# Griffin-style block on one core: another home for one weight load, and the scheduler's order for the block products on TensorE

## The chip, the cores and the metric

The kernel runs on one core of one Trainium2 chip. The metric is the device time of one execution in microseconds (us), lower is better; a run's figure is that of the core, and several runs are given as a median with their lowest and highest. The engines are TensorE (PE: matmuls; PEld is its weight load), VectorE (DVE), ScalarE (ACT), GpSimd (POOL) and SyncE (SP, which here issues the weight loads). Each has its own instruction stream and takes it in order; the streams wait for each other through semaphores.

## The reference

One layer of a streaming encoder, batch 1, 512 frames, width 1024, everything in float32:

```python
xn = rmsnorm(h, norm_mix_g[l])
u = jnp.einsum('bsd,de->bse', xn, w_in[l])
q, k, v, xr, gr, ga, gb = jnp.split(u, splits, axis=-1)
ya = chunked_band_attention(q, k, v, rel_table[l]) @ w_attn_out[l]
xc = causal_depthwise_conv(xr, conv_w[l], conv_b[l])
hr = rg_lru(xc, w_rg_r[l], b_rg_r[l], w_rg_i[l], b_rg_i[l], rg_lambda[l])
yb = (hr * jax.nn.gelu(gr)) @ w_rnn_out[l]
gates = jax.nn.sigmoid(jnp.concatenate([ga, gb], axis=-1) + b_merge[l])
g_a, g_b = jnp.split(gates, 2, axis=-1)
h = h + (g_a * ya + g_b * yb) @ w_o[l]
hn = rmsnorm(h, norm_ffn_g[l])
gu = hn @ w_ffn_in[l]
g, up = jnp.split(gu, 2, axis=-1)
h = h + (jax.nn.silu(g) * up) @ w_ffn_out[l]
return rmsnorm(h, final_norm_g)
```

The change lies in `gu = hn @ w_ffn_in`: 512 x 1024 times 1024 x 5632, that is 22 column tiles of 128 for the gate half (g) and 22 for the up half (u).

## The kernel before, in words

**Products.** Every float32 operand is split into a high part (an ACT copy to a rounded type, L80) and a low part (source minus high part on DVE, L81), in the function `split`. A product is then three matmuls per 128 rows of the contraction: high x high, high x low, low x high (`mm3`, L74 to L76).

**Stages in the order of time.** Norm and input projection, recurrence, attention, the merge into `mT`, the product with `w_o` (po_h), the second norm (`norm_half`), the first FFN column pair fg0 and fu0 done plainly (po_f), then the block products fg2, fu2, fg4, fu4 ... fg20, fu20, and the output product (po_out) with the final norm.

**Block products.** From the second pair of column tiles on, a 1024 x 256 piece of weights is cut into 2 x 2 blocks (a11, a21, a12, a22), and hn into b11, b12, b21, b22. Sums of weight blocks (s1 to s4, `weight_sums`, L175 to L181) and of hn blocks (t1 to t4, L971) let seven block products do the work of eight. Each is 4 x 3 = 12 matmuls of 128x256 (`product`). `block_product` issues the seven in this order, with two PSUM banks:

- p takes a11 x b11, and later, added onto it, s2 x t2, s3 x t3 and a22 x t4. Between them ACT copies the bank's running value out (`keep`, L274): twice into `keepa`, once into `keepb`, and at the end into c[:, 2].
- q holds two halves: a12 x b21 in the first; s1 x t1 and, on top of it, s4 x b22 in the second. After s1 ACT keeps the second half in `keepb`.
- DVE adds keeps and q into the result c (L286, L287). `keepa` and `keepb` are the two buffers of the tag `tg`, so the next block's keeps wait for these additions.

The order is p a11, q a12, p s2, q s1, p s3, q s4, p a22. A running value must be copied before the next product may write the bank. p has four buffers (tag mm, shared with po_f), q two for g and two for u.

After the g block, ACT applies silu to c (L1020); after the u block, DVE multiplies (L1022). Before the last pair (j = 20), `split_act(0)` starts splitting the finished activations for po_out (L1008 on ACT, L1009 on POOL).

**Weights.** `prefetch` and `weights` build a block's weights one block ahead in the program text. `load` (L137 to L152) brings a raw block of 512 KB by a DMA on SP, two per piece: `raw_fg_0` holds a11 and a21, `raw_fg_4` holds a12 and a22. Raw blocks live in the pool `wp`, tag raw, three buffers; every fourth load of the block products (L145) goes to the pool `sc` instead (`room[0]`), which has one buffer for it. The split blocks live in four buffers of `wp` plus one in `sums`, a22 in two of `sc`. For fg2 the sums are made early: `weight_sums("fg2", True)` loads both blocks once for the sums (loads 1 and 2), and later, after `sc` is opened, both blocks are loaded again for a11, a12 and a22 (loads 3 and 4); these three go to buffers of the pool `act`. Load 4, fg2's second raw block, therefore lies in `sc`. `sc` is opened after `x32` is closed and takes over its place, where a half of hn lies that po_f reads.

**Order.** A scheduler orders each engine's instructions when the program is built. Where the text stands in `tc.manual_schedule(engines={PE})`, TensorE keeps the order of the text; the loop over the block products (L1013 to L1022) stands in such a block. ACT, DVE and SP are ordered by the scheduler there too. Pools decide who waits: a tile waits until its buffer's last user is done.

Of the kernel before, what the change touches and what calls it, by code (L numbers as in the profile page):

```python
# [8 lines left out]
F32 = mybir.dt.float32  # L9
F32R = mybir.dt.float32r  # L10
AF = mybir.ActivationFunctionType
# [3 lines left out]
P = 128  # L15
# [7 lines left out]
FT = DFF // P  # L23
# [13 lines left out]
def block_kernel(ctx: ExitStack, tc: tile.TileContext, x, norm_mix_g, w_in, b_merge, rel_table,  # L37
# [3 lines left out]
    pe, dve, act, pool, sp = nc.tensor, nc.vector, nc.scalar, nc.gpsimd, nc.sync  # L41

    def pool_of(name, bufs=1, side="left"):
        return tc.tile_pool(name=name, bufs=bufs, side=side, reuse_waits="tile")

    def opened(name, bufs=1, side="left"):
        st = ExitStack()
        return st, st.enter_context(pool_of(name, bufs, side))
# [6 lines left out]
    wp = ctx.enter_context(pool_of("wp", 2))  # L55
# [10 lines left out]
    def f(ap):  # L66
        return ap.bitcast(F32)
# [69 lines left out]
    def load(name, k):  # L137
        _, parts, rows, kts = chunks[index[name]]
        wide = sum(width for *_, width in parts)
        n = min(4 * CW // wide, kts - k)  # L140
        at = rows + k * P
        pl, bufs = wp, 3
        if name in strassen and name[0] == "f":
            loads[0] += 1
            pl, bufs = (room[0], 1) if loads[0] % 4 == 0 else (wp, 3)  # L145
        raw = pl.tile([P, n, wide], F32, tag="raw", bufs=bufs, name=f"raw_{name}_{k}")
        to = 0
        for src, col, width in parts:
            sp.dma_start(out=raw[:, :, to:to + width],
                         in_=src[at:at + n * P, col:col + width].rearrange("(k p) e -> p k e", p=P))  # L150
            to += width
        raws[name, k] = raw  # L152

    slots, loads = [0], [0]
    barrier = ["wo1"]
    room = [None]
# [4 lines left out]
    def weight_sums(name, ahead=False):  # L161

        def blocks_of():
            for k in (0, 4):
                if (name, k) not in raws:
                    load(name, k)
            r0, r1 = raws.pop((name, 0)), raws.pop((name, 4))
            return r0[:, :, 0:P], r0[:, :, P:CW], r1[:, :, 0:P], r1[:, :, P:CW]
# [51 lines left out]
    def prefetch(n):  # L220
        while len(made) < min(n, len(chunks), index.get(barrier[0], len(chunks))):
            name, parts, rows, kts = chunks[len(made)]
            if name in strassen:
                made.append(weight_sums(name))
                continue
            tiles = []
            wide = sum(width for *_, width in parts)
            step = 4 * CW // wide
            for k in range(0, kts, step):
                n_ = min(step, kts - k)  # L230
                if name in extra:
                    hl = extra[name].tile([P, 2, n_, wide], F32R, tag="whl", bufs=4, name=f"whl_{name}_{k}")
                else:
                    hl = wp.tile([P, 2, n_, wide], F32R, tag="whl", bufs=4, name=f"whl_{name}_{k}")
                if (name, k) not in raws:
                    load(name, k)
                raw = raws.pop((name, k))
                split(hl[:, 0], hl[:, 1], raw[:])
                tiles.append(hl)
            made.append(lambda part, k, at, tiles=tiles, step=step: tiles[k // step][:, part, k % step, at])  # L240

    def weights(name, ahead=1):
        prefetch(index[name] + 1 + ahead)
        return made[index[name]]
# [10 lines left out]
    def right_side(blk_at, sums):  # L255
        out = {f"b{kh + 1}{half + 1}": lambda part, k, kh=kh, half=half: blk_at(kh, half, part, k)
               for kh in range(2) for half in range(2)}
        out.update({f"t{i + 1}": lambda part, k, i=i: sums[i][:, part, k] for i in range(4)})
        return out

    def product(o, w, b, start):

        for k in range(4):
            mm3(o, w[:, 0, k], w[:, 1, k], b(0, k), b(1, k), start and k == 0, k == 3, parts=True)

    def block_product(name, i, right, c):

        w = weights(name)
        p = ps.tile([P, 256], F32, tag="mm", bufs=4, name=f"p_{name}")
        q = ps.tile([P, 2, 256], F32, tag="st"[i % 2], bufs=2, name=f"q_{name}")  # L270
        a, b = (tg_.tile([P, 2, 256], F32, tag="tg", name=f"keep{n}_{name}") for n in "ab")

        def keep(o, src):
            act.activation(o, src, AF.Copy)  # L274

        product(p[:], w["a11"], right["b11"], True)
        keep(a[:, 0], p[:])
        product(q[:, 0], w["a12"], right["b21"], True)
        product(p[:], w["s2"], right["t2"], False)
        keep(a[:, 1], p[:])  # L280
        product(q[:, 1], w["s1"], right["t1"], True)
        keep(b[:, 0], q[:, 1])
        product(p[:], w["s3"], right["t3"], False)
        keep(b[:, 1], p[:])
        product(q[:, 1], w["s4"], right["b22"], False)
        dve.tensor_add(c[:, 3], b[:, 0], b[:, 1])  # L286
        dve.tensor_add(c[:, 0:2], q[:], a[:])  # L287
        product(p[:], w["a22"], right["t4"], False)
        keep(c[:, 2], p[:])
# [17 lines left out]
    warm = cp.tile([P, 1], F32, name="warm")  # L307
    act.activation(warm[:], eps_t[:], AF.Sqrt)
    load("xr0", 0)
    load("xr0", 4)  # L310
    for t in range(2, NT):
# [280 lines left out]
    def gelu_in(j, po_gr):  # L592

        g = rw.tile([P, S], F32, tag="g", name=f"g{j}")
        act.activation(g[:], po_gr[:], AF.Square, scale=(GELU_C * GELU_A) ** 0.5)
        dve.scalar_tensor_tensor(g[:], g[:], GELU_C, po_gr[:], ALU.add, ALU.mult)
        return g
# [77 lines left out]
    with tc.manual_schedule(engines={mybir.EngineType.Activation, mybir.EngineType.DVE}):  # L675
# [8 lines left out]
        g = [gelu_in(0, po[0])]  # L684
# [253 lines left out]
    def act_tile(j):  # L938
        o = acp.tile([P, 2, S], F32, tag="act", name=f"act{j}")
        act2.append(o)  # L940
        return o
# [40 lines left out]
    for i, t in enumerate((t1, t2, t3, t4)):  # L982
        o = btp.tile([P, 2, 4, 256], F32R, name=f"bt{i}")
# [3 lines left out]
    hn_right = right_side(lambda kh, half, part, k: bl[kh, half][:, part, k], bt)  # L987
    x32_stack.close()
    sc_stack, sc = opened("sc", 2)
# [13 lines left out]
    def split_act(i):  # L1003
        o = act2[i]
        pl, bufs = (acp, 13) if i == 0 else (ohp, 6) if i < 7 else (op, 4)
        hi = pl.tile([P, 2, S], F32R, tag="act", bufs=bufs, name=f"act_hi{i}")
        lo = acp.tile([P, 2, S], F32R, tag="act", bufs=13, name=f"act_lo{i}")
        act.activation(hi[:], o[:], AF.Copy)  # L1008
        (pool if i in (0, 1, 2, 4) else dve).tensor_sub(lo[:], o[:], f(hi[:]))  # L1009
        for c in range(2):  # L1010
            actT[2 * i + c] = (hi[:, c], lo[:, c])

    with tc.manual_schedule(engines={mybir.EngineType.PE}):  # L1013
        for j in range(2, FT, 2):
            if j == FT - 2:
                split_act(0)
            g, u = (sc.tile([P, 4, 256], F32, tag=f"c{w}", name=f"c_{w}{j}") for w in "gu")
            block_product(f"fg{j}", 0, hn_right, g)
            o = act_tile(j)[:].rearrange("p a b -> p (a b)")
            act.activation(o, g[:].rearrange("p a b -> p (a b)"), AF.Silu)  # L1020
            block_product(f"fu{j}", 1, hn_right, u)
            dve.tensor_mul(o, o, u[:].rearrange("p a b -> p (a b)"))  # L1022
    sc_stack.close()
    bt_stack.close()
    sums_stack.close()
# [100 lines left out]
```

## Time and profile before

| | us |
|---|---|
| median of 3 runs | 883.68 |
| lowest, highest | 883.22, 884.0 |
| the profiled execution's own time | 883.01 |
| its span, from the first to the last instruction | 881.2 |
| TensorE busy | 869.5 |
| VectorE busy | 552.1 |
| ScalarE busy | 475.4 |
| GpSimd busy | 113.6 |

The profile is that of one execution. Times within it count from the span's start. A row of a timeline gives start, duration, engine, line, operation, out<-in, shapes, and in brackets how long the engine stood idle before it and what ended that. Matmuls are pipelined: one that lasts 0.28 us is followed by the next after 0.12 us, so a gap shows in the distance between two starts. In a row by stretches there follow, after the stretch's length, busy time and number of instructions of PE, PEld, DVE, ACT and POOL, then the granted TensorE clock, the DMA share and GB/s. A row of groups gives count, busy time and mean ns, then the engine's idle time before these instructions and what ended it. The mean granted TensorE clock of the execution is 0.998.

### The profile page before, as it was taken

The numbers are of one execution on the slowest core, as the hardware profiler recorded it, in microseconds if no ns is written. First come the engines' busy times: TensorE is split into PE (matmuls) and PEld (weight loads), VectorE is DVE, ScalarE is ACT, GpSimd is POOL, SyncE is SP. The second block draws the span as 40 slices with busy tenths as digits, with TensorE's granted clock in tenths as the row PEclk, the third lists the DMA queues.
The fourth block names the chain that finished last, engine by engine and source line by source line (L and its number), as shares of the span: only waits on it lengthen the run. The fifth ranks groups of instructions, "written<-read, shape, count | busy, mean of one in ns | idle before, by whom it ended". The sixth has DMA issues, their size and how long they took to land.

```text
span 881.2 us, 13339 instructions
## 1 busy us (share of the span) xinstructions
PE 869.5 (99%) x5220; PEld 775.8 (88%) x5220; DVE 552.1 (63%) x843; ACT 475.4 (54%) x827; POOL 113.6 (13%) x172
## 2 busy tenths in 40 slices
PE   9999999999999999999999999999999999999997
PEld 7988888888889888898888889899999999888886
DVE  5676556663456675766556458888888885564203
ACT  7586556642257675766534366655565665723103
POOL 3512112120112131312000000000000000401100
PEclk9999999999999999999999999999999999999999
DMA  8133222433332332322224531433333332363002
GB/s 287 54 120 100 91 91 79 119 96 96 107 108 73 86 94 73 107 87 61 96 90 151 190 96 46 146 97 98 119 96 108 109 96 73 96 212 121 26 1 96
DMA packets 86143, 90.10 MB, mean 102 GB/s; under 512 B 5456, under 2 KB 74672, under 8 KB 86080
## 3 DMA queue, kind: packets, MB, share of 16 engines
q1 hardware_dynamic: 84480, 85.73, 31.5%
q10 hardware_dynamic: 1376, 3.47, 1.0%
q8 instruction: 41, 0.67, 0.3%
q14 instruction: 22, 0.18, 0.1%
q0 software_dynamic: 224, 0.05, 0.0%
HBM read 87.10 MB, written 2.14 MB: 101 GB/s over the span
## 4 chain that ended last, share of the span: by engine, by line
PE 94%; DVE 2%; DMA 1%; ACT 1%; POOL 1%; issue 1%; DVEq 0%; POOLq 0%; ACTq 0%
PE po_out L75 5%; PE po_out L76 5%; PE po_out L74 5%; PE p_fu L74 2%; PE p_fu L76 2%; PE p_fu L75 2%; PE p_fg L74 2%; PE p_fg L76 2%; PE p_fg L75 2%; PE pT L806 2%; PE o L826 2%; PE po_v L74 2%; PE po_v L76 2%; PE po_v L75 2%; PE po_xr L75 2%; PE po_xr L74 2%
## 5 line engine op out<-in xcount | busy, mean ns | idle before, releaser
L75 PE MATMUL po_out<-whl_fo,act_hi 128*128 128x512 f32 (+1 forms) x198 | 72.4, 366 | 0.0
L74 PE MATMUL po_out<-whl_fo,act_hi 128*128 128x512 f32 (+1 forms) x198 | 72.4, 366 | 0.0
L76 PE MATMUL po_out<-whl_fo,act_lo 128*128 128x512 f32 (+1 forms) x198 | 71.7, 366 | 0.0
L81 DVE TENSOR_TENSOR whl_fo<-raw_fo,whl_fo 128x1024 fp32r<-128x1024 f32 x22 | 28.8, 1317 | 49.1 <-ACT whl_fo L80 48.6
L795 POOL TENSOR_SCALAR p<-p,rl 128x128 f32<-128x128 f32 (+1 forms) x64 | 36.7, 592 | 134.6 <-DVE rl L793 134.3
L1009 POOL TENSOR_TENSOR act_lo<-act,act_hi 128x1024 fp32r<-128x1024 f32 x4 | 11.3, 2836 | 328.4 <-PE q_fu L76 298.8
L80 ACT ACTIVATE whl_fo<-raw_fo 128x1024 fp32r<-128x1024 f32 x22 | 23.1, 1058 | 47.2 <-PE po_out L76 31.1
L74 PEld LDWEIGHTS po_out<-whl_fo,act_hi 128*128 128x128 f32 x198 | 37.4, 189 | 6.0
L76 PEld LDWEIGHTS po_out<-whl_fo,act_lo 128*128 128x128 f32 x198 | 37.3, 189 | 6.0
L75 PEld LDWEIGHTS po_out<-whl_fo,act_hi 128*128 128x128 f32 x198 | 37.4, 189 | 6.0
L792 ACT ACTIVATE p<-p,m 128x128 f32<-128x128 f32 (+1 forms) x64 | 35.7, 560 | 12.1 <-DVE m L791 11.8
L74 PE MATMUL po_v<-whl_v,xnT 128*128 128x256 f32 x128 | 36.5, 285 | 0.0
L76 PE MATMUL po_v<-whl_v,xnT 128*128 128x256 f32 x128 | 36.2, 283 | 0.0
L75 PE MATMUL po_v<-whl_v,xnT 128*128 128x256 f32 x128 | 36.2, 283 | 0.0
L81 DVE TENSOR_TENSOR whl_fg_s<-s_fg,whl_fg_s 128x1024 fp32r<-128x1024 f32 x20 | 25.6, 1281 | 11.8 <-ACT whl_fg_s L80 11.8
L80 ACT ACTIVATE whl_fu_s<-s_fu 128x1024 fp32r<-128x1024 f32 x20 | 21.1, 1059 | 20.9 <-PE q_fg L76 9.5
L80 ACT ACTIVATE whl_fg_s<-s_fg 128x1024 fp32r<-128x1024 f32 x20 | 21.2, 1058 | 18.6 <-PE q_fg L76 9.5
L791 DVE CUSTOM_DVE_ANT_0 p<-s,bias 128x128 f32<-128x128 f32 (+1 forms) x64 | 29.1, 483 | 1.0 <-PE s L783 1.0
L81 DVE TENSOR_TENSOR whl_qk<-raw_qk,whl_qk 128x1024 fp32r<-128x1024 f32 x16 | 20.9, 1305 | 13.4 <-ACT whl_qk L80 13.4
L81 DVE TENSOR_TENSOR whl_fu_s<-s_fu,whl_fu_s 128x1024 fp32r<-128x1024 f32 x20 | 24.4, 1225 | 5.6 <-ACT whl_fu_s L80 5.3
L81 DVE TENSOR_TENSOR pp<-pT,pp 128x384 fp32r<-128x384 f32 (+1 forms) x48 | 27.5, 596 | 0.5 <-ACT pp L80 0.4
L75 PE MATMUL po_xr<-xnT,whl_xr 128*128 128x512 f32 (+1 forms) x80 | 27.7, 353 | 0.0
(428 smaller groups left out, 3070.2 us busy)
## 6 DMA issues: line engine op xcount, KB each, us to landing
raw_fg<-in_w_ffn_in_dram SPq DMA_DIRECT2D x24, 512.0 KB, 3.5
raw_fu<-in_w_ffn_in_dram SPq DMA_DIRECT2D x22, 512.0 KB, 3.5
raw_fo<-in_w_ffn_out_dram SPq DMA_DIRECT2D x22, 512.0 KB, 3.5
raw_qk<-in_w_in_dram SPq DMA_DIRECT2D x32, 256.0 KB, 3.2
raw_xr<-in_w_in_dram SPq DMA_DIRECT2D x8, 512.0 KB, 3.5
raw_gr<-in_w_in_dram SPq DMA_DIRECT2D x8, 512.0 KB, 3.5
raw_ga<-in_w_in_dram SPq DMA_DIRECT2D x8, 512.0 KB, 3.5
raw_gb<-in_w_in_dram SPq DMA_DIRECT2D x8, 512.0 KB, 3.5
```

The lines of the kernel that those rows point to most:

```text
L74: pe.matmul(o, sh, mh, start=start, stop=False, skip_group_check=parts)
L75: pe.matmul(o, sh, ml, start=False, stop=False, skip_group_check=parts)
L76: pe.matmul(o, sl, mh, start=False, stop=stop, skip_group_check=parts)
L80: act.activation(hi, src, AF.Copy)
L81: dve.tensor_sub(lo, src, f(hi))
L791: dve.tensor_tensor_reduce(prob[qb][:], scs[qb][:, 0:w], bias[:, S - w:S], -1.0, 3e38, ALU.add, ALU.min, nmax[:, qb:qb + 1])
L792: act.activation(prob[qb][:], prob[qb][:], AF.Exp, bias=nmax[:, qb:qb + 1], scale=-1.0, accum_out=lsum[:, qb:qb + 1])
L795: pool.tensor_scalar(prob[qb][:], prob[qb][:], rl[:, qb:qb + 1], 1.0, ALU.mult, ALU.mult)
L806: pe.transpose(pt[:, at * P:(at + 1) * P], prob[qb][:, kb * P:(kb + 1) * P], ident[:])
L826: pe.matmul(po[:, S - n:S], st, pp[i][:, part, lo:lo + n], start=kb == 0 and part == 0, stop=kb == NT - 1 and part == 1)
L1009: (pool if i in (0, 1, 2, 4) else dve).tensor_sub(lo[:], o[:], f(hi[:]))
```

## The change

Two edits. In `load`, the fourth load of the block products no longer goes to `sc`; it takes a buffer of `wp` like its neighbours. Loads 8, 12, 16 and so on go to `sc` as before. In the loop over the block products, `manual_schedule` goes, so that the scheduler orders TensorE there too; the body of the loop is the same.

```diff
@@ -142,7 +142,7 @@
         pl, bufs = wp, 3
         if name in strassen and name[0] == "f":
             loads[0] += 1
-            pl, bufs = (room[0], 1) if loads[0] % 4 == 0 else (wp, 3)
+            pl, bufs = (room[0], 1) if loads[0] % 4 == 0 and loads[0] > 4 else (wp, 3)
         raw = pl.tile([P, n, wide], F32, tag="raw", bufs=bufs, name=f"raw_{name}_{k}")
@@ -1010,16 +1010,15 @@
-    with tc.manual_schedule(engines={mybir.EngineType.PE}):
-        for j in range(2, FT, 2):
-            if j == FT - 2:
-                split_act(0)
-            g, u = (sc.tile([P, 4, 256], F32, tag=f"c{w}", name=f"c_{w}{j}") for w in "gu")
-            block_product(f"fg{j}", 0, hn_right, g)
...
+    for j in range(2, FT, 2):
+        if j == FT - 2:
+            split_act(0)
+        g, u = (sc.tile([P, 4, 256], F32, tag=f"c{w}", name=f"c_{w}{j}") for w in "gu")
+        block_product(f"fg{j}", 0, hn_right, g)
...
```

In the built program the number of instructions on each engine is the same. TensorE's order is the same up to the first block product and again from the end of the last one. In between, the products of two or three blocks are woven into each other, for instance at the start: fg2 p a11 (12 matmuls), fg2 q a12 (12), fg2 q s1 (12), fu2 p a11 (4), fg2 p s2 (12), fu2 p a11 (8), fu2 q a12 (9), fg2 q s4 (12). SP's loads at this place stood in the order fg2 first, fu2 first, fu2 second, fg4 first, fg2 second, fg4 second; now fg2 first, fg2 second, fu2 first, fu2 second, fg4 first, fg4 second. The orders of ACT and DVE change in the same stretch.

More of the change, by code (lines that the diff above doesn't have):

```diff
@@ L1011, in split_act @@
             actT[2 * i + c] = (hi[:, c], lo[:, c])
-    with tc.manual_schedule(engines={mybir.EngineType.PE}):
-        for j in range(2, FT, 2):
-            if j == FT - 2:
-                split_act(0)
-            g, u = (sc.tile([P, 4, 256], F32, tag=f"c{w}", name=f"c_{w}{j}") for w in "gu")
-            block_product(f"fg{j}", 0, hn_right, g)
[L1019 to L1022, printed above, removed]
+    for j in range(2, FT, 2):
[3 more added lines that the diff above has]
+        block_product(f"fg{j}", 0, hn_right, g)
+        o = act_tile(j)[:].rearrange("p a b -> p (a b)")
+        act.activation(o, g[:].rearrange("p a b -> p (a b)"), AF.Silu)
+        block_product(f"fu{j}", 1, hn_right, u)
+        dve.tensor_mul(o, o, u[:].rearrange("p a b -> p (a b)"))
     sc_stack.close()
```

## The prediction

> **What bounds the kernel now.** I read the page's shares first, then the chain that ended last, then TensorE's waits, then the block-product stage (549 to 753 us) in stretches, and at last the matmuls around each gap.
>
> ```profile
> span 881.2 us, 13339 instructions
> ...
> PE 869.5 (99%) x5220; PEld 775.8 (88%) x5220; DVE 552.1 (63%) x843; ACT 475.4 (54%) x827; POOL 113.6 (13%) x172
> ...
> PE 94%; DVE 2%; DMA 1%; ACT 1%; POOL 1%; issue 1%; DVEq 0%; POOLq 0%; ACTq 0%
> ```
>
> TensorE is busy 99% of the span and carries 94% of the chain. The edit removes no matmul, so it can only win where TensorE stands still. What it waited for (total, times, longest, in us), for the rows in this stage:
>
> ```profile
> PE q_fg L74 <- ACT whl_fg_a L80: 1.2, 1, 1.2
> ...
> PE p_fg L74 <- ACT keepa_fg L274: 0.7, 1, 0.7
> ...
> PE p_fu L74 <- ACT keepa_fu L274: 0.3, 1, 0.3
> PE q_fg L76 <- DVE whl_fg_a L81: 0.2, 1, 0.2
> ```
>
> Four waits, once each. Such waits understate the loss, because a matmul's modelled tail reaches into the gap. The distance between starts tells it better; so the stage by stretches (TensorE's count is the first x; the clock follows POOL):
>
> ```profile
> 538.00:549.00 11.00, 11.00 (x94) 11.00 (x93) 11.00 (x17) 8.15 (x13) 0.00 (x0) 1.00 0.16 49
> 549.00:559.00 10.00, 7.86 (x61) 7.25 (x60) 8.27 (x13) 5.55 (x10) 0.00 (x0) 1.00 0.58 181
> 600.00:650.00 50.00, 50.00 (x419) 50.00 (x418) 41.96 (x58) 30.12 (x53) 0.00 (x0) 1.00 0.34 106
> 726.00:728.00 2.00, 1.72 (x14) 1.51 (x13) 0.91 (x2) 1.75 (x3) 1.34 (x1) 1.00 0.00 0
> ```
>
> From 600 to 650 TensorE starts 419 matmuls, one per 50/419 = 0.119 us, with no gap: that is the pace at which nothing can be won. From 549 to 559 it starts 61 where the pace gives 84: 23 x 0.119 = 2.7 us lost. The gaps one by one:
>
> ```profile
> 550.59 0.28 PE L76 MATMUL p_fg<-hn,whl_fg_a 128*128 128x256 f32 x1
> 552.10 0.38 PE L74 MATMUL q_fg<-hn,whl_fg_a 128*128 128x256 f32 x1 [1.23 <-ACT whl_fg_a L80]
> 552.32 0.28 PE L75 MATMUL q_fg<-hn,whl_fg_a 128*128 128x256 f32 x1
> 552.83 0.39 PE L76 MATMUL q_fg<-hn,whl_fg_a 128*128 128x256 f32 x1 [0.22 <-DVE whl_fg_a L81]
> 553.05 0.28 PE L74 MATMUL q_fg<-hn,whl_fg_a 128*128 128x256 f32 x1
> ...
> 556.87 0.28 PE L76 MATMUL q_fg<-bt,whl_fg_s 128*128 128x256 f32 x1
> 557.84 0.39 PE L74 MATMUL p_fg<-bt,whl_fg_s 128*128 128x256 f32 x1 [0.69 <-ACT keepa_fg L274]
> 558.06 0.28 PE L75 MATMUL p_fg<-bt,whl_fg_s 128*128 128x256 f32 x1
> ...
> 726.29 0.28 PE L76 MATMUL q_fu<-hn,whl_fu_a 128*128 128x256 f32 x1
> 726.85 0.39 PE L74 MATMUL p_fu<-bt,whl_fu_s 128*128 128x256 f32 x1 [0.28 <-ACT keepa_fu L274]
> 727.07 0.28 PE L75 MATMUL p_fu<-bt,whl_fu_s 128*128 128x256 f32 x1
> ```
>
> Gap A, at fg2's second product: four steps from 550.59 to 553.05 take 2.46 us instead of 4 x 0.12 = 0.48: 1.98 us lost. Gap B, before fg2's s3 product: 556.87 to 558.06, two steps, 1.19 - 0.24 = 0.95. Gap C, before fu18's s2 product: 726.29 to 727.07, 0.78 - 0.24 = 0.54. Together **3.47 us**, all that this stage has to give.
>
> **The change: the load's home.** Why A exists:
>
> ```profile
> SPq L149 <- PE po_f L76: 5.5, 1, 5.5
> ...
> 548.02 0.37 SPq L149 DMA_DIRECT2D raw_fg<-in_w_ffn_in_dram  x1
> ...
> 551.42 1.15 ACT L80 ACTIVATE whl_fg_a<-raw_fg 128x512 fp32r<-128x512 f32 x2 [2.70 <-DMA raw_fg<-in_w_ffn_in_dram]
> ```
>
> fg2's second raw block lives in `sc`, which opens over tiles that po_f's last products still read; so its load is issued at 548.02 and ScalarE can split it at 551.42, when TensorE has wanted it since 550.71. The edit puts this load in `wp`, where the new SP order has it second, in front of fu2's two and fg4's first:
>
> ```profile
> 521.84 1.50 SPq L149 DMA_DIRECT2D raw_fu<-in_w_ffn_in_dram  x2
> 542.10 11.67 SPq L149 DMA_DIRECT2D raw_fg<-in_w_ffn_in_dram  x3
> ...
> 538.87 0.62 ACT L80 ACTIVATE whl_fg_a<-raw_fg 128x512 fp32r<-128x512 f32 x1
> ...
> 541.38 0.69 DVE L81 TENSOR_TENSOR whl_fg_a<-raw_fg,whl_fg_a 128x512 fp32r<-128x512 f32 x1
> ...
> raw_fg<-in_w_ffn_in_dram SPq DMA_DIRECT2D x24, 512.0 KB, 3.5
> ```
>
> It takes the slot of 521.84 and lands by 521.84 + 3.5 = 525.3. In the new orders ScalarE splits it right after 538.87, and VectorE has both low parts after its row of 541.38 and one sum: done by 541.38 + 4 x 0.69 = 544.1, six us before 550.59. A goes whole: -1.98.
>
> Three buffers serve this load, so something is pushed back: fu2's second block now waits for the buffer that the VectorE row of 541.38 frees, the issue that stands at 542.10 today. It lands at 545.6. Its first VectorE reader comes behind fg2's low part, a sum, two more low parts, two t's and one s split; at 0.69 and 1.23 us each that is 541.38 + 4 x 0.69 + 3 x 1.23 = 547.8. Cover 2.2 us; without it VectorE would slip, but TensorE needs that block's a12 only 60 matmuls after 549.3, near 556.4. Behind this wait on SP stand fg4's two loads: the first goes out when fg2's second block is split (544.1) and lands at 547.6, for a product 108 matmuls after 549.3, near 562. Cost 0.
>
> fg4's second block now has `sc` to itself and is issued at 548.02. ScalarE's new order has its a22 split in front of fg2's first keep, so that keep waits for the landing: 551.42 + 0.62 + 0.38 = 552.4. TensorE's new order puts 40 matmuls (a11, a12, s1, four of fu2's) ahead of the s2 product that needs it: 549.27 + 40 x 0.12 = 554.1. Cover 1.7 us; the old order would have wanted it after 24, at 552.1, and lost 0.3. Cost 0.
>
> **The change: TensorE's order.** Why B and C exist:
>
> ```profile
> 554.73 2.01 ACT L80 ACTIVATE whl_fu_s<-s_fu 128x1024 fp32r<-128x1024 f32 x2 [1.90 <-DVE s_fu L179]
> ...
> 724.53 1.05 ACT L1020 ACTIVATE act<-c_g 128x1024 f32<-128x1024 f32 x1
> 725.48 1.05 ACT L1008 ACTIVATE act_hi<-act 128x1024 fp32r<-128x1024 f32 x1
> 726.42 0.38 ACT L274 ACTIVATE keepa_fu<-p_fu 128x256 f32<-128x256 f32 x1
> ```
>
> The p bank holds a running sum: ScalarE must copy it (keep) before the next product may write. From the last p matmul the trip is 0.28 (matmul) + 0.38 (keep) + two handovers of 0.05 (726.42 + 0.38 = 726.80, TensorE at 726.85) = 0.76 us. The written order has one q product of 12 between, 13 x 0.12 = 1.56 us, so 0.80 is spare: less than one 1024-wide ScalarE row. Two such rows in front (the 2.01 of 554.73) made B; silu (L1020) and act_hi made C.
>
> In the changed program's order I counted the matmuls between a p product and the next one of its block: 24 or more everywhere (before: 12), only fu20's last has 16, four of them 512 wide. 25 x 0.12 = 3.0 us, spare 2.2: over two ScalarE rows. In front of B's s3 product there are now 31, in front of C's s2 product 36; silu and act_hi come behind that keep and in front of fu18's next one, which has 41. Both gaps go: -0.95 and -0.54.
>
> What gets tighter is the handover to the next block, because `tg` has two buffers: the next block's first keep waits until VectorE has added up the block before. From that block's s4 product to the next one's s2 product there were 36 matmuls; now 22 to 50, with 22 once and 24 twice, 31 or more elsewhere. Prices:
>
> ```profile
> L80 ACT ACTIVATE whl_fu_s<-s_fu 128x1024 fp32r<-128x1024 f32 x20 | 21.1, 1059 | 20.9 <-PE q_fg L76 9.5 <-PE q_fu L76 9.5 <-DVE s_fu L179 1.9
> ...
> L81 DVE TENSOR_TENSOR whl_fu_s<-s_fu,whl_fu_s 128x1024 fp32r<-128x1024 f32 x20 | 24.4, 1225 | 5.6 <-ACT whl_fu_s L80 5.3
> ...
> L287 DVE TENSOR_TENSOR c_g<-q_fg,keepa_fg 128x512 f32<-128x512 f32 x10 | 6.9, 692 | 2.5 <-PE q_fg L76 2.5
> ```
>
> The trip: 0.28 + 0.69 (the sum) + 0.38 + 3 x 0.05 = 1.50. At 22 matmuls 23 x 0.12 = 2.76 leaves 1.26: one foreign row on one engine fits (1.06 or 1.23), one on each (2.29) does not and would cost 1.03. At 31 it leaves 2.34 and even that fits. So the bounds for this edit are 0 and 3 x 1.03 = 3.1 us. I take 0: at all three the listed orders put no ScalarE split and at most one 512-wide VectorE sum between the s4 product's end and the keep.
>
> Switching between open sums seems free: from 538 to 549 the order of before already weaves two po_f sums in part, and the row shows 94 starts in 11 us, 0.117 each, no slower than 0.119. One start more or less in 94 is 1%, so over the stage's 1680 matmuls (200 us) the row bounds it to 2 us either way; I take 0, since the count is the same.
>
> **Sum.** The profiled execution took 883.01 us, 1.8 over its span and 0.67 under the median 883.68. 883.01 - 3.47 = 879.54; against the median 880.21. I predict **880.2**. A measurement of this kernel can tell about 0.2% (1.8 us) from no change.
>
> **Rivals.**
> *Only the home works.* A goes, but the scheduler's order brings new stalls worth B and C: 883.68 - 1.98 = 881.7. For it: three tight handovers, price up to 3.1. Against: 24 and more between keeps. Chance 0.10.
> *The gain is eaten.* fg4's keep or fu2's late block stalls by what A lost: within 1.8 us of 883.7. It needs a landing 1.7 us later than 551.42. Chance 0.06.
> *Slower: a keep behind a split that has no buffer.* Weight buffers live longer when blocks overlap, and ScalarE takes its work in order; it already stands 20.9 us in 20 such splits waiting for TensorE. Added to the trip with a row on each engine, one such wait (1.06) makes 1.50 + 2.29 + 1.06 = 4.85 us, against 32 x 0.12 = 3.84: 1.0 lost. It decides against the change from 3.47/19 = 0.18 us per handover on; with 0.5 at each of 19, 883.68 - 3.47 + 9.5 = 889.7. Against it: VectorE and ScalarE are busy 42.0 and 30.1 of 50 us, and these waits exist today without holding TensorE. Chance 0.10.
> *Slower by the clock.* Woven products could let TensorE's pace fall back for stretches. Its first matmuls, all 128x512, show a slower pace:
>
> ```profile
> 2.00:4.00 2.00, 2.00 (x6) 0.76 (x5) 0.00 (x0) 0.84 (x2) 1.90 (x4) 1.00 0.87 314
> 4.00:6.00 2.00, 2.00 (x9) 0.86 (x8) 0.19 (x2) 1.55 (x4) 2.00 (x5) 1.00 1.01 374
> ```
>
> 6 starts instead of 9 in 2 us: one relapse of that length costs 2 x 3/9 = 0.67 us; one per pair of blocks, ten, 6.7: 883.68 - 3.47 + 6.7 = 886.9. Against it: gaps A and B, 2.93 us, already account for the 2.7 missing from 549 to 559, so nothing is left for a slow pace even after the stage's longest stop. Chance 0.02.
> [...]
>
> **How the numbers follow.** Forecast 0.72 (879.4 to 881.2), home only 0.10, eaten 0.06, slower 0.12. Home only lies at the 0.2% bound (881.9), so half of it counts as same: faster 0.77, same 0.11, slower 0.12. The range runs from 879.4, the profiled sum less 0.1, to 883.3, the forecast plus the 3.1 of the three handovers; outside it stay the slower cases and part of the eaten one.
>
> **What would show it.** Right: the waits of q_fg on whl_fg_a and of p_fg and p_fu on their keeps gone; 549 to 559 with 83 or 84 matmuls; fg2's second block issued near 522, fg4's second near 548. Wrong: a new row in which p_fg or p_fu waits for a keep, ten or more times; fewer than 418 matmuls in 600 to 650; a granted clock under 1.00; or a wait of whl_fu_a on its DMA near 546.

## The result and the profile after

The changed kernel takes 879.9 us (median of 5 runs, 879.85 to 880.5), the kernel before 883.57 beside it (5 runs, 883.22 to 884.0). The ratio is 0.9959, with a 95% interval of 0.9947 to 0.9972: 3.67 us less, twice the 1.8 us that the prediction took as the least a measurement can tell from no change, and the interval lies below 1. Measured once more, it took 879.82 beside 883.49, 0.9959 (0.9945 to 0.9972).

The page of the kernel after, its first lines:

```profile
span 878.0 us, 13349 instructions
...
PE 868.9 (99%) x5220; PEld 775.8 (88%) x5220; DVE 545.3 (62%) x843; ACT 471.4 (54%) x827; POOL 115.1 (13%) x172
```

The span is 3.2 us shorter with the same 5220 matmuls. All that TensorE still waited for, in the whole program (total, times, longest):

```profile
PE busy L300 <- DVE eps_t L306: 1.2, 1, 1.2
PE pT L806 <- POOL p L795: 0.9, 3, 0.3
PE pt_mix_0t L466 <- DVE xs_mix L446: 0.5, 2, 0.3
PE po_xr L74 <- ACT xnT L468: 0.4, 2, 0.2
```

None lies in the block products: the four rows of q_fg, p_fg and p_fu are gone. By stretches:

```profile
549.00:559.00 10.00, 10.00 (x86) 10.00 (x85) 9.01 (x14) 4.72 (x8) 0.00 (x0) 1.00 0.37 107
600.00:650.00 50.00, 50.00 (x419) 50.00 (x418) 40.49 (x56) 29.55 (x53) 0.00 (x0) 1.00 0.34 107
...
726.00:728.00 2.00, 2.00 (x19) 2.00 (x18) 2.00 (x4) 2.00 (x4) 0.00 (x0) 1.00 0.00 0
```

86 matmuls stand where there were 61, and 19 where there were 14; from 600 to 650 there are 419 as before. No start from 540 to 757 comes more than 0.01 us later than the pace allows (0.119 us after a 256-wide matmul, 0.227 after a 512-wide one of po_out). The loads and the first two ScalarE rows that followed them:

```profile
520.27 2.10 SPq L149 DMA_DIRECT2D raw_fg<-in_w_ffn_in_dram  x2
523.14 19.54 SPq L149 DMA_DIRECT2D raw_fu<-in_w_ffn_in_dram  x2
544.11 0.92 SPq L149 DMA_DIRECT2D raw_fg<-in_w_ffn_in_dram  x2
```

```profile
550.24 0.63 ACT L80 ACTIVATE whl_fg_a<-raw_fg 128x512 fp32r<-128x512 f32 x1 [1.31 <-DMA raw_fg<-in_w_ffn_in_dram]
551.16 0.39 ACT L274 ACTIVATE keepa_fg<-p_fg 128x256 f32<-128x256 f32 x1 [0.29 <-PE p_fg L76]
```

fg2's second block goes out behind the first, by 522.4 (520.27 + 2.10). But both of fg4's go out by 544.11 + 0.92 = 545.0, the second not at 548.02 as I had predicted, and ScalarE does not hold up fg2's first keep at all.

### The profile page after: what moved, and what is told of

Read it like the earlier page. It is cut to its first block, busy times and chain, and to the rows that moved or that the text cites. A ratio compares the mean times of both kernels' runs of the same rounds, so it can differ in the third digit from the quotient of the medians.

```text
span 878.0 us, 13349 instructions
## 1 busy us (share of the span) xinstructions
PE 868.9 (99%) x5220; PEld 775.8 (88%) x5220; DVE 545.3 (62%) x843; ACT 471.4 (54%) x827; POOL 115.1 (13%) x172
## 3 DMA queue, kind: packets, MB, share of 16 engines
q10 hardware_dynamic: 1376, 3.47, 1.1%
## 4 chain that ended last, share of the span: by engine, by line
PE 95%; DVE 2%; POOL 1%; ACT 1%; issue 0%; DMA 0%; ACTq 0%; DVEq 0%; POOLq 0%
PE po_out L74 4%; PE po_out L76 4%; PE po_out L75 4%; PE p_fg L76 2%; PE p_fg L75 2%; PE p_fg L74 2%; PE p_fu L75 2%; PE p_fu L76 2%; PE p_fu L74 2%; PE pT L806 2%; PE o L826 2%; PE po_v L74 2%; PE po_v L76 2%; PE po_v L75 2%; PE po_xr L75 2%; PE po_xr L74 2%
## 5 line engine op out<-in xcount | busy, mean ns | idle before, releaser
L75 PE MATMUL po_xr<-xnT,whl_xr 128*128 128x512 f32 (+1 forms) x80 | 27.7, 353 | 0.0
L75 PE MATMUL po_gr<-xnT,whl_gr 128*128 128x512 f32 (+1 forms) x80 | 27.5, 347 | 0.0
L76 PE MATMUL po_gr<-xnT,whl_gr 128*128 128x512 f32 (+1 forms) x80 | 27.3, 347 | 0.0
L76 PE MATMUL po_xr<-xnT,whl_xr 128*128 128x512 f32 (+1 forms) x80 | 27.2, 346 | 0.0
```

What stands on the lines that cost most here:

```text
L75: pe.matmul(o, sh, ml, start=False, stop=False, skip_group_check=parts)
L76: pe.matmul(o, sl, mh, start=False, stop=stop, skip_group_check=parts)
```

## The experiments

In each, gaps are distances between TensorE's starts beyond the pace, from 540 to 757. The kernel before took 883.46 to 883.66 beside them.

**1. The home alone.**

```diff
-            pl, bufs = (room[0], 1) if loads[0] % 4 == 0 else (wp, 3)
+            pl, bufs = (room[0], 1) if loads[0] % 4 == 0 and loads[0] > 4 else (wp, 3)
```

> Only the load's new home; TensorE keeps the written order in the block products. Theory of the prediction (the home ends gap A, the order ends B and C): A gone, 883.57 - 1.98 = 881.6 us, B (0.95) and C (0.54) still there as waits of p_fg and p_fu on their keeps. Rival: B also came from the late load, because without it ScalarE's order has the two fu_s splits behind fg2's second keep; then A and B go with the home alone, only C stays, 883.57 - 1.98 - 0.95 = 880.6 us. Both expect fg2's second raw block to be issued near 522. If fg4's second block is issued near 544.5 as in the changed kernel, the written order does not lose the 0.3 us at fg2's first keep that the prediction gave for a landing at 551.42.

Measured 881.15 us beside 883.66, ratio 0.9971 (0.9959 to 0.9982). That lies between the two theories, so the trace must tell. ScalarE around the keep before fg2's last product, and around fu4's first keep:

```profile
557.12 1.05 ACT L80 ACTIVATE whl_fu_s<-s_fu 128x1024 fp32r<-128x1024 f32 x1
558.08 0.37 ACT L274 ACTIVATE keepb_fg<-p_fg 128x256 f32<-128x256 f32 x1
...
580.38 0.38 ACT L274 ACTIVATE c_g<-p_fg 128x256 f32<-128x256 f32 x1 [2.50 <-PE p_fg L76]
580.66 1.05 ACT L80 ACTIVATE whl_fg_s<-s_fg 128x1024 fp32r<-128x1024 f32 x1
581.61 0.62 ACT L80 ACTIVATE whl_fg_a<-raw_fg 128x512 fp32r<-128x512 f32 x1
582.13 1.05 ACT L1020 ACTIVATE act<-c_g 128x1024 f32<-128x1024 f32 x1
583.08 0.37 ACT L274 ACTIVATE keepa_fu<-p_fu 128x256 f32<-128x256 f32 x1
```

The two fu_s splits of gap B are apart now. The gap of 0.95 at fg2's s3 product is gone; one fu_s split stands in front of the keep at 558.08, and 0.17 is lost at the a22 product that needs it. C is there with its 0.54. And a gap D is new, 0.54 at fu4's first keep (583.08), by the rows because whl_fg_s now comes behind the c copy; in the kernel before it started at 581.17 and the copy at 582.61. No run takes D alone. From the changed kernel upwards, 879.9 + 0.17 + 0.54 + 0.54 = 881.15. So the rival is right about B, and both missed D.

**2. The order alone.** `manual_schedule` goes, and the load stays in `sc`.

> Only the scheduler's order of TensorE; fg2's second raw block stays in sc, so it is issued near 548 and split near 551.4. Theory of the prediction (A needs the home): B and C gone, A stays at about 1.98, 883.57 - 1.49 = 882.1 us. Rival (the order alone covers the late load): the order puts fu2's first two products, 24 matmuls or 2.9 us, in front of fg2 q a12, which is then needed near 553.6 instead of 550.7, after the split that ends near 552.7; A, B and C all gone, about 880.0 us, as fast as both edits together.

Measured 880.13 beside 883.66, ratio 0.9959 (0.9947 to 0.9972). The late load is as late as ever; ScalarE, then TensorE at the first and the third matmul of fg2's q a12, with the start of s2 between:

```profile
551.84 1.15 ACT L80 ACTIVATE whl_fg_a<-raw_fg 128x512 fp32r<-128x512 f32 x2 [2.73 <-DMA raw_fg<-in_w_ffn_in_dram]
```

```profile
553.97 0.28 PE L74 MATMUL q_fg<-hn,whl_fg_a 128*128 128x256 f32 x1
...
554.21 0.28 PE L74 MATMUL p_fg<-bt,whl_fg_s 128*128 128x256 f32 x1
...
555.65 0.28 PE L76 MATMUL q_fg<-hn,whl_fg_a 128*128 128x256 f32 x1
```

TensorE does fu2's first two products first and comes to q a12 at 553.97, 1.0 us after the split has ended (552.99); even between the matmuls of q a12 it finds other work while VectorE makes the low part. No row carries a wait; A, B and C are all gone. The rival is right: the order alone covers the late load. There is no gap up to 757 at all. From the first matmul of the block products to the kernel's last matmul (start to start) it is 549.65 to 871.85 here, 322.20 us, and 549.47 to 871.64 in the changed kernel, 322.17: where the edits act, the two are equally fast. This profile reaches that stretch 0.18 later, and the 0.23 us between 880.13 and 879.9 are no gap of the order's.

**3. C by itself.** The home, the written order, and the activation split asked for one block product later.

```diff
-            if j == FT - 2:
-                split_act(0)
             g, u = (sc.tile([P, 4, 256], F32, tag=f"c{w}", name=f"c_{w}{j}") for w in "gu")
...
+            if j == FT - 2:
+                split_act(0)
             block_product(f"fu{j}", 1, hn_right, u)
```

> The home with the written order, and the split of the finished activations (split_act(0)) asked for one block product later, between fg20's and fu20's, so that act_hi no longer stands in front of fu18's keep. Theory (C is two 1024-wide ScalarE rows, silu and act_hi, in front of one keep; one alone, 1.05, would use up the 0.80 us spare by 0.25 at most): gap C (0.54) is gone or at most 0.25, so 0.3 to 0.5 us below e1_home_only. Rival 1: the same two rows now stand in front of a keep of fu20 and the 0.54 comes back there; the time of e1_home_only within 0.1. Rival 2: C has nothing to do with act_hi and stays at fu18.

Measured 880.62, ratio 0.9965 (0.9952 to 0.9977), 0.53 under the home alone. Of its waits of p_fu two had been there, of 0.3 each; one is left, D:

```profile
PE p_fu L74 <- ACT keepa_fu L274: 0.3, 1, 0.3
```

C is what the prediction took it for: two 1024-wide ScalarE rows in front of one keep, with 12 matmuls to cover them. With one of them moved, it is gone. The same two rows, silu and act_hi, now stand in front of fu20's first keep, as the first rival said (742.40 and 743.36, the keep done at 744.67); there TensorE also does six matmuls of po_out and wants the keep at 746.05, so nothing is lost.

**4. Why fg4's load was early.** The changed kernel, with a tile of tag raw allocated first in `sc`, and never used.

```diff
     room[0] = sc
+    sc.tile([P, 4, CW], F32, tag="raw", bufs=1, name="raw_first")
```

> The changed kernel with one edit that computes nothing: right after sc is opened a tile of its tag raw is allocated and never used, so that this tag gets its place in sc ahead of all others, as it had in the kernel before. In the changed kernel fg4's second block was issued at 544.5 and not at 548.02 as predicted. Theory (the place of the tag in sc decides: in the old place it lies over the half of hn that po_f reads last): fg4's second block is issued near 548.0, lands near 551.4, ScalarE's first keep of fg2 moves from 551.16 to about 552.4, and TensorE still does not wait, because it needs that keep only at 554.1: 879.9 us, within 0.2 of the changed kernel. Rival (the issue time hangs on SP's order or on the split before it, not on the place): issue stays near 544.5. Second rival (the cover of 1.7 us was wrong): a wait of p_fg on its keep appears, and the time rises by some tenths.

Measured 879.96 beside 883.66, ratio 0.9957 (0.9943 to 0.9971). SP's two loads of fg4, then ScalarE, then TensorE at the s2 product:

```profile
544.33 4.48 SPq L149 DMA_DIRECT2D raw_fg<-in_w_ffn_in_dram  x2
```

```profile
552.16 0.63 ACT L80 ACTIVATE whl_fg_a<-raw_fg 128x512 fp32r<-128x512 f32 x1 [3.02 <-DMA raw_fg<-in_w_ffn_in_dram]
552.70 0.37 ACT L274 ACTIVATE keepa_fg<-p_fg 128x256 f32<-128x256 f32 x1
```

```profile
554.49 0.28 PE L74 MATMUL p_fg<-bt,whl_fg_s 128*128 128x256 f32 x1
```

The pair now ends at 544.33 + 4.48 = 548.8, so the second was issued near 548.4. The place of the tag in the new pool decides when the buffer is free. In the kernel before, the first allocation in `sc` was this raw block, which lay over tiles that po_f still read; with load 4 gone to `wp`, a22 is the first, and fg4's block lies where nothing is read any longer. With the early place taken away the keep ends at 553.07, and TensorE wants it at 554.49: the cover that I had predicted is there (1.4 us; 1.7 predicted), and it was not needed.

**5. The same late block under the written order.** Edit 4 on top of the home alone.

> The new home with the written order, and the unused first tile of tag raw in sc as in e6_raw_first_woven, where fg4's second block was issued at 548.44 and its a22 split, in front of fg2's first keep, started at 552.16. Theory (step of the prediction: the written order wants this keep after 24 matmuls, near 552.1 to 552.6, and so loses by a late fg4 block what the woven order covers): the keep ends near 553.1, TensorE waits for it 0.3 to 0.7 us more than in e1_home_only, 881.4 to 881.9 us. Rival (the order of ScalarE comes out differently or DVE is the late one): within 0.15 us of e1_home_only, 881.15.

Measured 881.49 beside 883.49, ratio 0.9976 (0.9967 to 0.9985): 0.34 over the home alone by the medians, 0.5 by the differences to the kernel before. TensorE at fg2's s2 product:

```profile
552.21 0.28 PE L76 MATMUL q_fg<-hn,whl_fg_a 128*128 128x256 f32 x1
552.72 0.39 PE L74 MATMUL p_fg<-bt,whl_fg_s 128*128 128x256 f32 x1 [0.23 <-ACT keepa_fg L274]
552.94 0.28 PE L75 MATMUL p_fg<-bt,whl_fg_s 128*128 128x256 f32 x1
```

Two steps take 0.73 instead of 0.24: 0.49 lost at a place where the woven order lost nothing. With 4 it compares the two orders most cleanly: a late keep of the same kind, with 28 matmuls between a11 and s2 in the one and 12 in the other.

**6. and 7. How much reserve.** Every keep done three times, in the written and in the changed order.

```diff
         def keep(o, src):
-            act.activation(o, src, AF.Copy)
+            for _ in range(3):
+                act.activation(o, src, AF.Copy)
```

> Every keep is done three times over (the same copy, so the result is the same), with the new home and the written order of TensorE: about 0.55 us more per keep on ScalarE (two rows behind another at 0.27). It measures how much reserve an order has. Theory (the reserve between two products on one bank is what the order changes): with 12 matmuls between, 0.80 us of reserve shrinks to 0.25, and in front of the first keep of each u block stands silu (1.05) behind a c copy that is now also tripled; some 0.8 us lost at each of the ten, plus smaller losses at other keeps: 8 to 16 us over e1_home_only, 889 to 897 us, with p_fg and p_fu waiting for keeps ten times and more. Rival (TensorE's own pace and not the reserve sets the time, the gaps of before were accidents of three places): under 1 us over e1_home_only, about 882.

> The changed kernel with every keep done three times over, as in e4_keep3_written. Theory (reserve): 24 and more matmuls between two products of one bank leave 2.2 - 0.55 = 1.65 us of reserve, still over one 1024-wide ScalarE row, so at most a few gaps: 880 to 882 us, and the distance to e4_keep3_written is 8 us or more. Rival (load on ScalarE decides: some 100 keeps more than twice 0.27 us each put 55 us on an engine that is busy 59% of the stage, which makes 86%): woven and written orders rise alike, 8 us and more each.

Measured 923.32 (ratio 1.0451, 1.0436 to 1.0465) and 905.64 (1.0248, 1.0234 to 1.0262): 42.2 over the home alone, 25.8 over the changed kernel. For the written order neither theory comes near. For the other, the distance of more than 8 us came as the theory said, but both orders lose more than 8, as the rival said, though not alike. In the written order p_fu alone waits nine times for its keep, 14.6 us in all. ScalarE at one of them:

```profile
612.84 0.38 ACT L275 ACTIVATE keepa_fu<-p_fu 128x256 f32<-128x256 f32 x1
613.10 1.06 ACT L1021 ACTIVATE act<-c_g 128x1024 f32<-128x1024 f32 x1
614.05 0.38 ACT L275 ACTIVATE keepa_fu<-p_fu 128x256 f32<-128x256 f32 x1
614.31 1.06 ACT L80 ACTIVATE whl_fg_s<-s_fg 128x1024 fp32r<-128x1024 f32 x1
615.26 0.39 ACT L275 ACTIVATE keepa_fu<-p_fu 128x256 f32<-128x256 f32 x1
```

The three copies are not one long row. The scheduler put silu and a split between them, so this keep takes from 612.84 to 615.65, 2.8 us, not the 0.93 of my estimate. The woven order loses 16 us less, which speaks for reserve, but it too stops at keeps, for 2.5 to 3.4 us at three places, and its order was made anew for these rows. How much reserve the changed order has cannot be read from this pair.

**8. An overlap written out by hand.** The home, and the blocks woven in one fixed pattern.

```diff
+        product(q[:, 1], w["s1"], right["t1"], True)
+        keep(b[:, 0], q[:, 1])
+        yield
+        product(p[:], w["s2"], right["t2"], False)
...
+            for i, w in enumerate("gu"):
...
+                run = block_product(f"f{w}{j}", i, hn_right, c, (j, w) == (FT - 2, "u"))
+                if before:
+                    next(before[0])
+                next(run)
+                next(run)
+                if before:
+                    finish(before)
...
```

> The new home, and a third order of TensorE, written out by hand in place of the scheduler's: two neighbouring blocks overlap in one fixed pattern, s3 of the block before, a11, s1, a22 of the block before, s2, a12, s4. Between two products on the same p bank lie 24 matmuls everywhere but at the two ends (fg2 a11 to s2 12, fu20 s3 to a22 12), between s1 and s4 36. Theory (the distance does it, whoever makes it: 24 matmuls leave 2.2 us where 12 leave 0.80): no waits of p_fg and p_fu on keeps, 419 matmuls in 600 to 650, 879.8 to 880.2 us, as fast as the changed kernel. Rival (the scheduler's order works because it was planned together with ScalarE's; a regular overlap puts splits that wait for a weight buffer in front of keeps): a gap recurs in every pair, 0.3 us or more at each of ten to twenty blocks, 883 to 890 us.

> The same hand-written overlap with fg2's second raw block still in sc. Its splits (a12 and a22, from about 551.4 to 552.6) stand in front of fg2's first keep on ScalarE, and in this order only the 12 matmuls of s1 lie between a11 and s2 at fg2, so s2 is wanted near 552.2 and the keep is done near 553.0. Theory (a late load is covered by the matmuls that lie between, here 12): 0.8 us lost at this one place, 880.7 us if e9_hand_woven is 879.9; e2_order_only, with 40 and more matmuls there, lost nothing by the same load. Rival (late load costs a wait of q_fg on whl_fg_a as in the kernel before, 1.98): 881.9 us. Rival (nothing lost): as e9_hand_woven.

In these two kernels the product s1 x t1 is missing from c[:, 1] in every block (the output that shows it is told at the end); the instructions are all there. With the old home it took 880.75 (ratio 0.9968, 0.9957 to 0.998), as the theory said: one gap of 0.94, at fg2's s2, where 12 matmuls are too few for the late block. Everywhere but at the two ends 24 lie between there, and fu18 meets the two rows of gap C again: silu from 725.82, act_hi from 726.78, the keep done at 728.09, and TensorE wants it at 729.00. With the new home it took 883.35 (0.999, 0.9982 to 0.9999), which is neither theory: its eleven executions fall into two groups, five of 881.74 to 882.05 and six of 883.35 to 883.54. The profile is of the second; ScalarE, TensorE and the stretches:

```profile
554.18 0.38 ACT L274 ACTIVATE keepa_fg<-p_fg 128x256 f32<-128x256 f32 x1 [2.44 <-PE p_fg L76]
554.46 1.14 ACT L80 ACTIVATE whl_fg_a<-raw_fg 128x512 fp32r<-128x512 f32 x2
555.50 0.37 ACT L274 ACTIVATE keepb_fg<-q_fg 128x256 f32<-128x256 f32 x1
```

```profile
553.86 0.28 PE L76 MATMUL p_fg<-bt,whl_fg_s 128*128 128x256 f32 x1
555.92 0.47 PE L74 MATMUL q_fg<-hn,whl_fg_a 128*128 128x256 f32 x1 [1.78 <-ACT keepb_fg L274]
```

```profile
555.90:557.90 2.00, 1.98 (x9) 1.98 (x10) 2.00 (x3) 1.77 (x2) 0.00 (x0) 0.54 0.41 139
557.90:559.50 1.60, 1.60 (x9) 1.60 (x9) 0.24 (x1) 0.20 (x1) 0.00 (x0) 0.50 0.67 204
559.50:562.00 2.50, 2.50 (x23) 2.50 (x23) 1.41 (x2) 0.00 (x0) 0.00 (x0) 1.00 0.23 79
```

s1, which keepb copies, was finished before s2 began, but keepb stood behind the second keepa, which waits for s2, and behind two splits; a12 writes the same bank and waited for keepb. 1.94 are lost. Behind this stop the granted clock is half for 3.6 us, and the 18 matmuls in it take 0.21 each: about 1.6 us more, the distance of the two groups. After 560 there is no gap up to 757. So the pattern by hand holds the pace through nineteen blocks, and its start does not.

**9. A better pattern by hand.** a11, a12, s1, s2, then a22 of the block before, s4, s3.

> The new home and a second hand-written overlap of TensorE in the block products: a11, a12, s1, s2, then a22 of the block before, s4, s3. Between two products on one p bank lie 24 matmuls (48 before a22), between s1 and s4 24; only at the two ends it is 12 to 18. a12 stands before s1 in every block, so no product starts a sum in the bank's other half between s1 and s4. Theory (distance does it, whoever makes it): no start off the pace of 0.119 from 549 to 753 but at fg2's s3 or s4 perhaps a tenth; 879.8 to 880.2 us, as fast as the changed kernel (879.82). Rival (ScalarE's order at the start again puts a split in front of a keep, as the two splits of fg4 in front of keepb in e9_hand_woven, 1.94 and sometimes 1.6 more): 881.8 to 883.4 us.

> The same hand-written overlap with fg2's second raw block still in sc. a12 is fg2's second product here, as in the kernel before, so nothing lies between its due time, 550.7, and the split that starts near 551.7. Theory (a late load costs what is not covered by the matmuls in between, here none): gap A comes back, 1.9 to 2.1 us, plus 0 to 0.6 where two fu_s splits and one of fg4 stand in front of fg2's next keeps; 881.8 to 882.6 us if e13_hand_woven_a12_first is 879.9. Rival (an overlap by itself absorbs the late load, as the scheduler's order did in e2_order_only): 880.0 us. Rival (the stop makes TensorE's clock fall as the stop of 1.9 us did in e9_hand_woven): 1.6 us more in some executions, and a granted clock of about 0.5 for some 3.5 us in the profile.

With the new home, 880.03 beside 883.46, ratio 0.996 (0.9948 to 0.9973), and no gap at all. Its stretches:

```profile
549.00:559.00 10.00, 10.00 (x86) 10.00 (x85) 8.27 (x13) 4.89 (x10) 0.00 (x0) 1.00 0.36 109
...
600.00:650.00 50.00, 50.00 (x419) 50.00 (x418) 42.29 (x58) 30.20 (x54) 0.00 (x0) 1.00 0.37 108
```

That is as fast as the scheduler's order: in both, where 24 matmuls or more lie between two products on one bank, and the weights are there in time, the pace holds (419 matmuls from 600 to 650), whoever wrote the order. With the old home this pattern takes 883.04 (0.9992, 0.9983 to 1.0001). TensorE and the stretches:

```profile
550.91 0.28 PE L76 MATMUL p_fg<-hn,whl_fg_a 128*128 128x256 f32 x1
552.44 0.39 PE L74 MATMUL q_fg<-hn,whl_fg_a 128*128 128x256 f32 x1 [1.25 <-ACT whl_fg_a L80]
...
553.17 0.39 PE L76 MATMUL q_fg<-hn,whl_fg_a 128*128 128x256 f32 x1 [0.23 <-DVE whl_fg_a L81]
553.39 0.28 PE L74 MATMUL q_fg<-hn,whl_fg_a 128*128 128x256 f32 x1
```

```profile
554.20:557.60 3.40, 3.40 (x19) 3.40 (x18) 2.93 (x5) 2.40 (x3) 0.00 (x0) 0.52 0.68 197
```

Gap A is back in its old size, 2.48 - 0.48 = 2.0, and the clock falls for 3.4 us: 16 matmuls at 0.094 more each are 1.5. 879.9 + 2.0 + 1.5 = 883.4 is the profiled execution's 883.36. Executions without the fall would be nearer 882; they read 882.7 and more. An estimate for them: at full pace s4 would be due near 557.3, and keepb ends at 558.1, which costs 0.8, hidden in the profiled one by the slow matmuls. No profile of such an execution shows it.

## Why the prediction was right, and where its steps were not

**The sum, right.** Gaps A, B and C, 3.47 us, were all that the stage had to give, and all of it came: 3.67 by the medians, 880.2 predicted and 879.9 measured. From the first matmul of the block products to the kernel's last matmul it was 549.27 to 874.90, 325.63 us, and is 549.47 to 871.64, 322.17: 3.46 less. (The two profiled executions differ by 3.13, partly because the one after began this stretch 0.20 later.) The total did not hang on which edit fills which gap, as both were made. The pace was read rightly, 419 matmuls per 50 us before and after.

**"A to the home, B and C to the order", wrong as a split.** The step took each gap for the property of one edit. The order alone takes all three (experiment 2), because 24 other matmuls stand in front of the late product; the home alone takes A and most of B, since without the late load ScalarE's order changes too, and it brings D, which only the written order with the new home has. The gains are not terms to be added: 2.51 and 3.53 alone, 3.67 together. Of the three gaps only C needs the order. On top of the home the order is worth 1.2. On top of the order the medians give the home 0.1 to 0.2 and the traces 0.03 (322.20 against 322.17), which these runs cannot tell from nothing.

**"Two such rows made B", one row short.** In the kernel before, a third row stood between the two fu_s splits and the keep of 557.42:

```profile
556.88 0.63 ACT L80 ACTIVATE whl_fg_a<-raw_fg 128x512 fp32r<-128x512 f32 x1
```

It puts the keep off by 557.42 - 556.88 = 0.54, so by this estimate more than half of B's 0.95 is this split's. The remedy, more matmuls in between, was right all the same.

**"Only the home works", a rival with the wrong reason.** Its 881.7 is near the 881.15 of experiment 1, but that kernel leaves the order out; the scheduler's order brought no stall in this stage.

**fg4's second block, wrong in time, right in cost.** I carried 548.02 over from the load that had stood in this buffer. The issue time belonged to the buffer's place, not to the pool (experiment 4). The cover of 1.7 for the case that did not happen is 1.4 by experiment 4, and the old order's loss of 0.3 in it is 0.49 by experiment 5: both steps hold, the second put too low.

**fu2's second block, right.** It was issued near 542.3 (542.1 predicted), and VectorE's first sum of it ran at 547.40 (547.8 predicted), with no idle time in front.

**Handovers at nothing, right, but not by the path that was priced.** There is no gap at any of the nineteen. The prediction let the next block's first keep wait for the sum behind s4 of the block before. At the three tight handovers (22 and twice 24 matmuls) it does not; VectorE and ScalarE at the first of them, from fu6 to fg8:

```profile
610.09 0.43 DVE L286 TENSOR_TENSOR c_u<-keepb_fu 128x256 f32<-128x256 f32 x1 [0.82 <-ACT keepb_fu L274]
610.55 0.38 ACT L274 ACTIVATE keepa_fg<-p_fg 128x256 f32<-128x256 f32 x1 [0.49 <-DVE c_u L286]
611.12 0.69 DVE L287 TENSOR_TENSOR c_u<-q_fu,keepa_fu 128x512 f32<-128x512 f32 x1 [0.60 <-PE q_fu L76]
```

The keep starts behind the other sum (L286), which frees the other buffer, and before the sum behind s4 (L287). It is done at 610.93, and TensorE wants it at 613.79. The keep is done 2.86, 2.86 and 3.16 us ahead at the three, and 2.29 or more at every handover, so the 3.1 that the prediction set above its forecast was never near.

**Weaving at nothing, right.** The pace is the same with products woven into each other: 419 matmuls from 600 to 650 in the scheduler's pattern and in that of experiment 9, and no gap from 560 to 757 in that of experiment 8.

**The clock, right here, and not negligible.** The changed kernel cycles through more open sums at a granted clock of 1.00 in every stretch read above. Experiment 9 with the new home cycles as much and does not lose the clock either: 1.00 from 549 to 559 and from 600 to 650. Where the clock was lost in this stage (0.50 in experiment 7, 0.50 to 0.54 in 8, 0.52 in 9 with the old home), it was behind a stop, of 2.47, 1.94 and 2.0 us.

## What to carry to other kernels

Where an engine works through a chain of sums that another engine must copy out, count the work between two links and compare it with the trip plus the longest rows that can stand in front of the copy; silu and act_hi, two wide rows of 1.05 us, cost 0.54 us where 12 matmuls lay between, and nothing where 24 did (experiment 8, old home: the keep done 0.91 us ahead). Such distance also absorbed the late load (experiment 2: A, 1.98 us, gone without the home), so try it before the loads, and do not add up the gains of edits that fill the same gaps. After moving a tile out of a pool, look again at what now lies first in it.

## What the runs showed of the hardware that I had not expected

**A stop of two microseconds can cost three and a half.** In experiment 8 a stop of 1.94, in experiment 9 one of 2.0, was followed by 3.4 to 3.6 us at a granted clock of about half, 1.5 to 1.6 us more; in the profiled execution of the kernel before, gap A of 1.98 was not, with a clock of 1.00 from 549 to 559, and in experiment 8 five of eleven executions seem spared. Length alone does not decide either. In experiment 7 the changed order's profile has stops of 2.70 (from 607.23), 3.42 (from 665.16) and 2.47 us (from 722.39). Behind the first two the clock is 1.00, behind the third:

```profile
725.30:728.70 3.40, 3.40 (x18) 3.40 (x17) 1.62 (x4) 1.72 (x5) 0.00 (x0) 0.50 0.02 5
```

Other executions of the kernel before may have lost the clock behind gap A: of the 56 beside the experiments, all 15 with a mean clock of 0.996 or 0.997 took 883.82 us or more, and all 29 with 0.999 or 1.0 took 883.74 or less. No profile of such an execution shows where. What decides it, no run here shows: one and the same program has both outcomes (experiment 8, by its two groups of times), and a stop of 1.94 us was followed by a slow stretch where one of 3.42 was not.

**A sum begun in one half of a bank, and a term gone from the other.** In experiment 8, where a12 starts its sum in one half of q's bank between s1 and s4 in the other, s4 replaced s1 x t1 instead of adding to it: the output of both kernels of that experiment lies 0.69884 of the norm from the reference's, and so does the reference computed without exactly this term in every block. In the other kernels a12 is begun before s1, and the term is there. How the start of one sum reaches the other half, no run here shows.

**Two loads side by side took longer.** The median time from issue to landing of this load was 3.5 us in the kernel before, and 3.4 for the one issued at 548.02 there. In the changed kernel fg4's two went out 0.5 us apart; the row of the tile's answer for 543 to 552:

```profile
DMA to landing us min/median/max: 4.3/5.0/5.7
```

One took 4.3 and the other 5.7, which ate half of the 3.9 us that the earlier issue had gained (544.5 against 548.4): ScalarE began the split at 550.24 here and at 552.16 in experiment 4.
